# When the third chunk's down groups are woven into quarters 8 to 10: eight weight loads two units later, in both layers

## The chip, the cores and the metric

The kernel runs on one core of a Trainium2 chip. Five engines work from instruction queues of their own: TensorE (PE; its weight loads are shown as PEld), VectorE (DVE), ScalarE (ACT), GpSimd (POOL) and SyncE (SP, which here only issues DMAs). The metric is the time of one launch in microseconds (us) on the device.

## The reference

Two layers over a sequence of 256 tokens and 2048 channels, in float32. Layer 0 mixes tokens by causal pooling, layer 1 by dilated causal attention; each is followed by a layer norm, a gated feed-forward network with a causal convolution of width 3, and another layer norm. The change touches the feed-forward part of both layers and, a little, the attention's mask.

```
def conv_ffn(h, w_up, conv_w, conv_b, w_down):
    u = h @ w_up
    up = jnp.pad(u, ((0, 0), (CONV_WIDTH - 1, 0), (0, 0)))
    c = conv_b + up[:, 0:S] * conv_w[0]
    for j in range(1, CONV_WIDTH):
        c = c + up[:, j:j + S] * conv_w[j]
    gate, val = jnp.split(c, 2, axis=-1)
    return (jax.nn.silu(gate) * val) @ w_down
```

The inner width is 5504 columns. The attention has three branches, of window and dilation (128, 1), (512, 4) and (2048, 16); a mask says which of a query's keys each branch reads.

## The kernel before

**Numbers.** Every float32 weight is taken apart into a high part (wh, an ACT copy with rounding) and a low part (wl, a DVE subtraction), and so are the activations. A product is then the sum of three products of parts. This is called a split here, and each load of weights (raw, 1 MB from HBM) needs one: `do_split`, lines 82 and 83.

**Units.** The program is a list of units, each one load of weights with its matmuls. `run_units` walks the list: for unit i it issues the load of unit i+5 on SP (there are 3 buffers for raw weights, so a load waits until DVE has finished with an older one), emits the splits up to unit i+3 on ACT and DVE (4 buffers), then the unit's matmuls, then whatever earlier units left for "n units later" (`later`), then what follows the end of a group (`post`). Each engine works its queue in that order, so a DVE instruction that waits holds every later one on DVE.

**Up units.** The inner width is cut into quarters of 512 columns, 0 to 10; quarter 10 has 384. A quarter's gates are a group of four up units (`up`, over four blocks of 512 input rows), and its values another four. PE multiplies with lines 165 and 166. At a group's end DVE and ACT take the sums out of PSUM (`evac`, lines 578 and 579), ACT and DVE work the convolution's taps (lines 587, 592 and 593), and after the values DVE multiplies with the gates (line 684), splits the product (gq, lines 286 and 290) and makes sums of its blocks (`left_sums`, lines 646 to 660).

**Down units.** The down projection runs in four chunks of quarters: 0 to 2, 3 to 5, 6 and 7, and 8 to 10. For a chunk there are four down groups, one for each 512 output columns. Where the quarter has block sums (in chunk three both 6 and 7 have), one load serves a Strassen-like product of seven block products instead of eight. Such a load makes a pair of units "a" and "b", here called one K unit: PE works 42 matmuls with lines 227 to 229, and `split_sums` needs lines 103 to 109 for the first half and 96 and 97 for the second. At the end of a down group `early_post` and `tm_post` take its sums out of PSUM (lines 825 to 858), and POOL adds three pieces to the stream HT in SBUF by accumulating DMAs (line 271). In layer 0 a DVE transpose of HT follows three units after a down group of the third chunk (`to_features`, line 811), and then 16 small DMAs on SP.

**Weaving.** `weave` puts the K units of a down group between the up units of a group. In the third chunk a down group has two K units (quarters 6 and 7), and they follow the second and the fourth up unit. The four down groups go with the values of 8, the gates and values of 9, and the gates of 10. The product of quarter 9 is held back until the last K unit is done (`free[9]`), since its buffers belong to quarters 6 and 7. In layer 1 the last chunk needs the block sums of quarter 9 as well, at once with its second unit.

**The mask.** In the attention stage `masks(i)` makes block i of two small tables, 128 by 128 each, with one POOL iota and ten DVE instructions, 7, 8 and 9 units after the stage's start. Blocks 0 and 2 are the same.

Of the kernel before, what the change touches and what calls it, by code (L numbers as in the profile page):

```python
# [32 lines left out]
def trunk(ctx: ExitStack, tc: tile.TileContext, x, pool_w_in, pool_w_grp, pool_scale, pool_w_out,  # L33
# [3 lines left out]
    V, A, PE = nc.vector, nc.scalar, nc.tensor  # L37
# [14 lines left out]
    units = []  # L52
# [243 lines left out]
    H, XC, XP, ST = {}, {}, {}, {}  # L296
# [251 lines left out]
    def ffn(lay):  # L548
# [153 lines left out]
        def up(q):  # L702
            nb = min(4, NF - 4 * q)
            x0 = q == 0
            mode = "x" if x0 else "ab"
            mark = len(units)
            group(w_up, rows4, 512 * q, nb * P, psrcs if x0 else xsrcs, gate_post(q, nb, mode),
                  mode=mode)
            group(w_up, rows4, FF + 512 * q, nb * P, xsrcs, val_post(q, nb, "ab"))
            us = units[mark:]  # L710
            del units[mark:]
            return us[:4], us[4:]

        def weave(us, ks):
            items = []
            for k in ks:
                if len(k) > 3 and k[3] == "b":
                    items[-1].append(k)
                else:
                    items.append([k])  # L720
            ends = []
            for i, u in enumerate(us):
                units.append(u)
                j = i - 1 if len(items) > 2 else (i - 1) // 2 if i % 2 else -1
                if j >= 0:
                    units.extend(items[j])
                    ends.append(len(units) - 1)
            return ends

        def down(n, last):  # L730
# [16 lines left out]
        for n in (0, 1):  # L747
            d = down(n, False)
            q = chunks[n + 1][0]
            ends = [weave(us, ks) for us, ks in zip(up(q) + up(q + 1), d)]  # L750
# [3 lines left out]
                for us in up(q + 2):  # L754
                    units.extend(us)
        d = down(2, False)
        gates8, vals8 = up(8)
        units.extend(gates8)
        gates10, vals10 = up(10)
        for us, ks in zip((vals8,) + up(9) + (gates10,), d):  # L760
            free[9] = weave(us, ks)[-1]
        units.extend(vals10)
        mark = len(units)
        if lay == 0:
            rows = [(512 * q, min(512, FF - 512 * q)) for q in (8, 9, 10)]
# [76 lines left out]
    def tm_post(lay, n, c):  # L842
# [92 lines left out]
        return post  # L935

    ffn(0)
    marks.append(len(units))

# [215 lines left out]
    with tc.tile_pool(name="attn", bufs=1) as ap:  # L1155
        pools["attn"] = ap
        for nm in ("cnt", "negm"):
            ST[nm] = ap.tile([P, 3, P], F32, name=nm)

        def masks(i):  # L1160
            two = ap.tile([P, 2, P], F32, name="dist", tag="t1", bufs=2)
            dist, fm = two[:, 0], two[:, 1]
            nc.gpsimd.iota(dist, pattern=[[-1, P]], base=P * (i == 1), channel_multiplier=1,
                           allow_small_or_imprecise_dtypes=True)
            itwo = ap.tile([P, 2, P], I32, name="idist", tag="t1", bufs=2)
            idist, im = itwo[:, 0], itwo[:, 1]
            cn = ST["cnt"][:, i, :]
            V.tensor_copy(idist, dist)
            V.tensor_scalar(cn, dist, float(P), None, op0=OP.is_le)
            for dil in (4, 16):  # L1170
                V.tensor_scalar(im, idist, dil - 1, None, op0=OP.bitwise_and)
                V.tensor_copy(fm, im)
                V.scalar_tensor_tensor(cn, fm, 0.0, cn, op0=OP.is_equal, op1=OP.add)
            V.scalar_tensor_tensor(cn, dist, 0.0, cn, op0=OP.is_ge, op1=OP.mult)
            V.tensor_scalar(ST["negm"][:, i, :], cn, 0.0, NEG, op0=OP.is_equal, op1=OP.mult)

        for i in range(3):
            later(7 + i, lambda i=i: masks(i))
        run_units(marks[2])
    with tc.tile_pool(name="ffn1", bufs=4) as fp:  # L1180
# [31 lines left out]
```

## Time and profile before

| | |
|---|---|
| median of three runs | 2059.56 us (2056.8 to 2061.82) |
| the profiled execution | 2057.01 us |
| its span, first to last instruction | 2055.2 us |
| PE busy | 2027.2 us |
| DVE busy | 1687.6 us |
| ACT busy | 1257.2 us |
| mean granted clock of PE | 0.998 |
| layer 0, quarters 8 to 10 | 698.9 to 877 us of the span |
| layer 1, quarters 8 to 10 | 1811 to 1983.5 us of the span |

The engines' lines give busy time over the whole span. A line of the waits says who waited, for whom, how long in total, how often, and the longest in us. A line of the timeline has start, length, engine, source line, operation and names (out<-in), and in brackets the idle time ahead of it and who ended it. A line of the window table has a stretch, its length, and for each engine its busy time and instructions; then the share of the clock that PE was granted, and the DMA's share and rate.

### The profile page before, as it was taken

The page shows a single profiled execution, that of the slowest core. Times are in us where ns is not written, and L with a number is a line of the kernel's source. Part 1 is how long each engine was busy: PE and PEld are TensorE (multiplying, and loading weights), DVE is VectorE, ACT ScalarE, POOL GpSimd, SP SyncE. Part 2 cuts the span into 40 slices and gives each one's busy share as a digit, 9 for nine tenths or more (in the row PEclk, how much of TensorE's full clock was granted, in tenths as well). Part 3 has the DMA queues.
Part 4 walks back from the last instruction along what each step waited for, and adds up shares of the span by engine and source line. Part 5 has one row for each costly group of instructions (what it writes and reads, how often), then busy time and mean ns, then how long its engine had stood idle before and what let it go on. Part 6 is the DMA issues. An engine that isn't in the chain of part 4 may idle for free. (4 is left out here: it accounts for less than half of the span.)

```text
span 2055.2 us, 31252 instructions
## 1 busy us (share of the span) xinstructions
PE 2027.2 (99%) x12532; PEld 1810.4 (88%) x12532; DVE 1687.6 (82%) x2020; ACT 1257.2 (61%) x1689; POOL 75.2 (4%) x112
## 2 busy tenths in 40 slices
PE   9999999999999999999999999999999999999998
PEld 8999988899899988889888888998899888988987
DVE  6768877898889899889856667787889888988989
ACT  6445687666766675657444444477666677657663
POOL 2000000000000100100000000000001000000100
PEclk9999999999999999999999999999999999999999
DMA  8655567556666647775566555557666756656665
GB/s 272 211 186 191 172 200 212 193 191 221 195 195 211 207 167 197 220 231 172 167 217 191 176 176 166 183 185 226 184 197 191 228 185 196 206 193 199 196 211 184
DMA packets 278305, 405.92 MB, mean 198 GB/s; under 512 B 80414, under 2 KB 95668, under 8 KB 277904
## 3 DMA queue, kind: packets, MB, share of 16 engines
q1 hardware_dynamic: 266144, 389.72, 57.5%
q0 software_dynamic: 11584, 13.55, 4.4%
q8 instruction: 98, 1.61, 0.3%
q10 hardware_dynamic: 432, 0.66, 0.1%
q14 instruction: 47, 0.39, 0.1%
HBM read 380.01 MB, written 2.10 MB: 186 GB/s over the span
## 5 line engine op out<-in xcount | busy, mean ns | idle before, releaser
L165 PE MATMUL acc<-xc,wh 128*128 128x512 f32 x3264 | 1155.8, 396 | 2.2 <-DVE o L1061 1.2
L166 PE MATMUL acc<-xc,wl 128*128 128x256 f32 x3264 | 918.9, 282 | 12.1 <-DVE wl L83 12.1
L83 DVE TENSOR_TENSOR wl<-raw,wh 128x2048 fp32r<-128x2048 f32 (+2 forms) x318 | 687.6, 2168 | 259.5 <-ACT wh L82 257.4
L165 PEld LDWEIGHTS acc<-xc,wh 128*128 128x128 f32 x3264 | 617.4, 189 | 146.1 <-DVE o L1061 1.9
L82 ACT CAST wh<-raw 128x2048 fp32r<-128x2048 f32 (+2 forms) x318 | 573.0, 1809 | 195.0 <-PE acc L165 110.0
L166 PEld LDWEIGHTS acc<-xc,wl 128*128 128x128 f32 x3264 | 616.9, 189 | 16.3 <-DVE wl L83 15.8
L96 ACT CAST wh<-raw 128x1024 fp32r<-128x1024 f32 x116 | 121.7, 1053 | 153.8 <-DVE raw L107 133.5
L97 DVE TENSOR_TENSOR wl<-raw,wh 128x1024 fp32r<-128x1024 f32 x116 | 138.9, 1222 | 1.1 <-ACT wh L96 1.1
L103 ACT CAST wh<-raw 128x1024 fp32r<-128x1024 f32 x116 | 90.6, 830 | 41.7 <-DMA raw<-in_ffn_w_down_dram 27.3
L106 DVE TENSOR_TENSOR wl<-raw,wh 128x1024 fp32r<-128x1024 f32 x116 | 105.6, 952 | 3.0 <-ACT wh L103 2.6
L578 ACT COPY ut<-acc 128x256 f32<-128x256 f32 x164 | 52.9, 372 | 80.2 <-DVE u L579 60.2
L587 ACT ACTIVATE c<-u,cv 128x256 f32<-128x256 f32 x172 | 89.5, 594 | 19.1 <-DVE f L650 9.0
L227 PE MATMUL t<-wh,g 128*128 128x256 f32 x344 | 96.8, 282 | 0.0
L228 PE MATMUL t<-wl,g 128*128 128x256 f32 x344 | 96.7, 281 | 0.0
L229 PE MATMUL t<-wh,g 128*128 128x256 f32 x344 | 96.3, 280 | 0.0
L228 PE MATMUL s<-wl,xs 128*128 128x256 f32 x308 | 86.2, 280 | 2.2 <-DVE wl L97 2.2
L229 PE MATMUL s<-wh,xs 128*128 128x256 f32 x308 | 85.9, 279 | 0.0
L227 PE MATMUL s<-wh,xs 128*128 128x256 f32 x308 | 85.8, 279 | 0.0
L271 POOL DMA_DIRECT2D ht<-w x24 | 20.3, 847 | 1756.9 <-ACT wh L103 950.4
L592 ACT ACTIVATE a<-u,cv 128x256 f32<-128x256 f32 x172 | 73.5, 500 | 15.9 <-DVE g L660 6.5
L592 ACT ACTIVATE u<-u,cv 128x256 f32<-128x256 f32 x172 | 73.5, 499 | 0.0
L109 DVE TENSOR_TENSOR raw<-raw 128x1024 f32<-128x1024 f32 x58 | 71.1, 1225 | 2.0
(276 smaller groups left out, 3432.9 us busy)
## 6 DMA issues: line engine op xcount, KB each, us to landing
raw<-in_ffn_w_up_dram SPq DMA_DIRECT2D x160, 1024.0 KB, 4.9
raw<-in_ffn_w_down_dram SPq DMA_DIRECT2D x80, 1024.0 KB, 5.2
raw<-in_pool_w_out_dram SPq DMA_DIRECT2D x16, 1024.0 KB, 5.0
raw<-in_shared_w_k_dram SPq DMA_DIRECT2D x16, 1024.0 KB, 5.0
raw<-in_attn_w_q_dram SPq DMA_DIRECT2D x16, 1024.0 KB, 5.4
raw<-in_shared_w_v_dram SPq DMA_DIRECT2D x16, 1024.0 KB, 5.4
raw<-in_attn_w_o_dram SPq DMA_DIRECT2D x16, 1024.0 KB, 5.0
raw<-in_pool_w_in_dram SPq DMA_DIRECT2D x12, 1024.0 KB, 5.9
```

Source lines behind the costliest of these rows:

```text
L82: A.copy(wh[i][:, s], r[:, s])
L83: V.tensor_tensor(wl[i][:, s], r[:, s], wh[i][:, s].bitcast(F32), OP.subtract)
L96: A.copy(h[:, :, n], r[:, :, n])
L97: V.tensor_tensor(l[:, :, n], r[:, :, n], h[:, :, n].bitcast(F32), OP.subtract)
L103: A.copy(h[:, k, n], r[:, k, n])
L106: V.tensor_tensor(l[:, k, n], r[:, k, n], h[:, k, n].bitcast(F32), OP.subtract)
L165: PE.matmul(ps[m], h[:, k, c], q[:, k, :, :T], start=st, stop=False)
L166: PE.matmul(ps[m][:, :T], l[:, k, c], q[:, k, 0, :T], start=False, stop=sp and not shifted)
L227: PE.matmul(to, xh, h[:, k, n], start=opens and kk == 0, stop=False)
L228: PE.matmul(to, xh, l[:, k, n], start=False, stop=False)
L229: PE.matmul(to, xl, h[:, k, n], start=False, stop=ends and kk == 1)
L592: A.activation(to[:, m, :], u[:, m, i:i + T], AF.Copy, scale=cv[:, i, j:j + 1])
```

## The change

The weave of a down group of two K units now puts them ahead of the first and of the third up unit instead of behind the second and the fourth. Quarter 8's gates and values run without any K unit, and the four down groups go with the gates and values of 9 and of 10. The chunks of three items (chunks one and two) keep their order. In the attention stage the third mask block is no longer computed, but copied from the first by two ACT copies.

```diff
+            def put(item):
+                units.extend(item)
+                ends.append(len(units) - 1)
+
             for i, u in enumerate(us):
+                if len(items) == 2 and i % 2 == 0:
+                    put(items[i // 2])
                 units.append(u)
-                j = i - 1 if len(items) > 2 else (i - 1) // 2 if i % 2 else -1
-                if j >= 0:
-                    units.extend(items[j])
-                    ends.append(len(units) - 1)
+                if len(items) > 2 and i > 0:
+                    put(items[i - 1])
             return ends
...
         d = down(2, False)
-        gates8, vals8 = up(8)
-        units.extend(gates8)
-        gates10, vals10 = up(10)
-        for us, ks in zip((vals8,) + up(9) + (gates10,), d):
+        for us in up(8):
+            units.extend(us)
+        for us, ks in zip(up(9) + up(10), d):
             free[9] = weave(us, ks)[-1]
-        units.extend(vals10)
...
+            if i == 0:
+                for nm in ("cnt", "negm"):
+                    A.copy(ST[nm][:, 2, :], ST[nm][:, 0, :])
+
-        for i in range(3):
+        for i in range(2):
             later(7 + i, lambda i=i: masks(i))
```

On SP, where quarter 8 of layer 0 begins to be loaded, the loads stood so before (raw is the buffer of one unit's weights, w_up an up unit, w_down a K unit):

```order
L72 DMA raw_6849<-in_ffn_w_up_dram 128x4x512
L72 DMA raw_6907<-in_ffn_w_up_dram 128x4x512
L72 DMA raw_6961<-in_ffn_w_down_dram 128x4x512
L72 DMA raw_7051<-in_ffn_w_up_dram 128x4x512
L72 DMA raw_7114<-in_ffn_w_up_dram 128x4x512
L72 DMA raw_7163<-in_ffn_w_down_dram 128x4x512
```

and stand so now, from the same load on:

```order
L72 DMA raw_6849<-in_ffn_w_up_dram 128x4x512
L72 DMA raw_6907<-in_ffn_w_up_dram 128x4x512
L72 DMA raw_6961<-in_ffn_w_up_dram 128x4x512
L72 DMA raw_7005<-in_ffn_w_up_dram 128x4x512
L72 DMA raw_7053<-in_ffn_w_down_dram 128x4x512
L72 DMA raw_7156<-in_ffn_w_up_dram 128x4x512
L72 DMA raw_7205<-in_ffn_w_up_dram 128x4x512
L72 DMA raw_7250<-in_ffn_w_down_dram 128x4x512
```

The first K unit's load stands two loads of w_up later; from there on one K load follows every two up loads, as before.

On DVE, around the K unit in the middle of quarter 10's gates in layer 0, this stood before (wl is a low part of weights, c a convolution's sum, w and u the down group's pieces on their way to ht):

```order
L109 TENSOR_TENSOR raw_7994<-raw_7994 128x4x256
L593 TENSOR_TENSOR c<-c,a 128x1024
L826 TENSOR_TENSOR w<-w,s_7885 128x256
L827 TENSOR_TENSOR u_8120<-w,s_7886 128x256
L831 TENSOR_TENSOR w<-w,s_7886 128x256
L832 TENSOR_TENSOR u_8124<-u_8120,s_7886 128x256
L853 TENSOR_TENSOR ht<-ht,t_7883 128x512
L858 TENSOR_TENSOR ht<-ht,t_7884 128x256
L97 TENSOR_TENSOR wl_8135<-raw_7994,wh_8134 128x4x256 x2
L593 TENSOR_TENSOR c<-c,u 128x1024
L684 TENSOR_TENSOR c<-c 128x1024
L83 TENSOR_TENSOR wl_8176<-raw_8078,wh_8175 128x1536
```

and this stands there now, with the transpose that comes ahead of the K unit:

```order
L814 STREAM_TRANSPOSE hb<-ht 128x2x4x128
L104 TENSOR_TENSOR raw_7917<-raw_7917 128x2x256
L106 TENSOR_TENSOR wl_8005<-raw_7917,wh_8004 128x4x256
L106 TENSOR_TENSOR wl_8005<-raw_7917,wh_8004 128x2x256
L107 TENSOR_TENSOR raw_7917<-raw_7917 128x2x256
L109 TENSOR_TENSOR raw_7917<-raw_7917 128x4x256
L593 TENSOR_TENSOR c<-c,a 128x1024
L97 TENSOR_TENSOR wl_8053<-raw_7917,wh_8052 128x4x256 x2
L593 TENSOR_TENSOR c<-c,u 128x1024
L684 TENSOR_TENSOR c<-c 128x1024
L83 TENSOR_TENSOR wl_8099<-raw_8002,wh_8098 128x1536
```

The six instructions that take a down group out of PSUM (lines 826 to 858) are gone from between the two halves of this K unit's split; the transpose (line 811, in the new file 814) stood behind the next up splits and now stands ahead of the first half. Those six instructions now stand in the K unit between the gates of 10 and its neighbours, on DVE ahead of its second half:

```order
L109 TENSOR_TENSOR raw_7763<-raw_7763 128x4x256
L829 TENSOR_TENSOR w<-w,s_7634 128x256
L830 TENSOR_TENSOR u_7865<-w,s_7635 128x256
L834 TENSOR_TENSOR w<-w,s_7635 128x256
L835 TENSOR_TENSOR u_7869<-u_7865,s_7635 128x256
L856 TENSOR_TENSOR ht<-ht,t_7632 128x512
L861 TENSOR_TENSOR ht<-ht,t_7633 128x256
L97 TENSOR_TENSOR wl_7880<-raw_7763,wh_7879 128x4x256 x2
L83 TENSOR_TENSOR wl_7920<-raw_7829,wh_7919 128x1536
```

The instructions are the same, their numbers of lines in the new file are higher by three.

## The prediction

> **What bounds the kernel now.** I read the page's first part, then PE's waits in the two stretches that the change re-orders, then the clock there, and last the order of time on DVE where PE waits.
>
> ```profile
> span 2055.2 us, 31252 instructions
> PE 2027.2 (99%) x12532; PEld 1810.4 (88%) x12532; DVE 1687.6 (82%) x2020; ACT 1257.2 (61%) x1689; POOL 75.2 (4%) x112
> ```
>
> PE works 2027.2 of 2055.2 us. The change keeps every matmul, so all it can move is in the 28 us of idle time and in slow matmuls. The next two fences are PE's waits from the first up unit of quarter 8 on, in layer 0 (698.86 to 877 us) and in layer 1 (1811 to 1984 us); columns are us in total, times, longest.
>
> ```profile
> PE acc L166 <- DVE wl L83: 5.1, 3, 2.0
> PE s L228 <- DVE wl L97: 2.0, 3, 1.6
> PE s L227 <- DVE u L579: 1.6, 1, 1.6
> PE acc L165 <- ACT wh L82: 0.5, 1, 0.5
> ```
> ```profile
> PE acc L166 <- DVE wl L83: 5.3, 4, 1.8
> PE s L227 <- DVE u L579: 1.5, 1, 1.5
> PE acc L165 <- ACT wh L82: 0.5, 1, 0.5
> PE s L228 <- DVE wl L97: 0.2, 1, 0.2
> ```
>
> That is 9.2 and 7.5 us: more than half of PE's idle time lies in these two stretches, nearly all of it behind DVE's splits of weights (wl). Two stretches of half clock come on top (window table: stretch, length, busy PE, PEld, DVE, ACT, POOL, granted clock, DMA):
>
> ```profile
> 743.60:747.00 3.40, 3.40 (x13) 2.92 (x12) 3.40 (x3) 3.24 (x7) 0.00 (x0) 0.50 0.87 307
> 846.00:849.40 3.40, 3.40 (x13) 2.82 (x12) 2.75 (x4) 1.57 (x2) 0.00 (x0) 0.50 0.83 249
> 1854.90:1858.30 3.40, 3.40 (x20) 3.00 (x21) 3.40 (x3) 3.40 (x7) 0.00 (x0) 1.00 0.70 235
> ```
>
> Each costs half of its 3.4 us and counts as busy: 3.4 us together, in layer 0 alone; the third row, behind layer 1's longest wait, keeps the full clock. Just ahead of the second one PE does this:
>
> ```profile
> 845.30 0.39 PE L166 MATMUL acc<-xc,wl 128*128 128x256 f32 x1 [1.98 <-DVE wl L83]
> 845.53 0.40 PE L165 MATMUL acc<-xc,wh 128*128 128x512 f32 x1
> ```
>
> The first matmul lasts 0.39 us but the next starts 0.23 after it; matmuls overlap by 0.16 us, and each wait loses that beside its idle time. With 8 waits in layer 0 the pool is 9.2 + 3.4 + 8 x 0.16 = 13.9 us, with 7 in layer 1 it is 7.5 + 1.1 = 8.6 us; 22.5 us in all.
>
> **Why PE waits there.** DVE in layer 0 around the K unit that now follows the second up unit of quarter 10's gates:
>
> ```profile
> 830.31 0.69 DVE L104 TENSOR_TENSOR raw<-raw 128x512 f32<-128x512 f32 x1 [2.06 <-DMA raw<-in_ffn_w_down_dram]
> ...
> 835.12 1.22 DVE L593 TENSOR_TENSOR c<-c,a 128x1024 f32<-128x1024 f32 x1
> 836.25 0.41 DVE L826 TENSOR_TENSOR w<-w,s 128x256 f32<-128x256 f32 x1
> ...
> 838.83 2.35 DVE L97 TENSOR_TENSOR wl<-raw,wh 128x1024 fp32r<-128x1024 f32 x2
> 841.10 1.22 DVE L593 TENSOR_TENSOR c<-c,u 128x1024 f32<-128x1024 f32 x1
> 842.35 1.23 DVE L684 TENSOR_TENSOR c<-c 128x1024 f32<-128x1024 f32 x1
> 843.50 3.42 DVE L83 TENSOR_TENSOR wl<-raw,wh 128x1536 fp32r<-128x1536 f32 x2
> ```
>
> The weights land at 830.3 after DVE sat idle for 2.06 us; from there DVE runs without a pause: first half's split (to 835.1), a tap, the evacuation of the down group that ended one K unit earlier (836.25 to 838.83, 2.58 us), the second half's split, tap, product, and the split for the next up unit, ready only at 845.2, which is where PE stood. So the K unit in mid-group carries two chains at once; the one between groups carries no evacuation. Unit lengths on PE (two up units, two small ones of quarter 10, one K unit):
>
> ```profile
> 760.37:771.61 11.24, 11.24 (x67) 9.81 (x66) 11.03 (x15) 9.85 (x17) 1.56 (x3) 1.00 0.36 122
> 827.54:835.96 8.42, 8.42 (x51) 7.35 (x49) 5.92 (x7) 6.12 (x11) 0.00 (x0) 1.00 0.77 238
> 771.61:776.55 4.94, 4.94 (x45) 4.94 (x43) 4.91 (x4) 2.00 (x2) 1.03 (x2) 1.00 1.03 223
> ```
>
> So 5.62, 4.21 and 4.94 us. Two more of DVE's prices, quarter 10's up split and the transpose, grouped by form from 760 to 860 us (busy us, mean ns | idle before):
>
> ```profile
> L83 DVE TENSOR_TENSOR wl<-raw,wh 128x1536 fp32r<-128x1536 f32 x6 | 10.5, 1756 | 2.6 <-ACT wh L82 2.5
> L811 DVE STREAM_TRANSPOSE hb<-ht 128x1024 f32<-128x1024 f32 x3 | 3.7, 1242 | 0.7 <-issue 0.7
> ```
>
> **The change, part by part.** The up units keep their order (quarters 8, 9, 10, gates then values). Each of the eight K units of the third chunk moves two up units later, in both layers. Nothing is added or removed on PE. On SP each K unit's load of 1 MB moves behind two loads of w_up, in layer 0 the 16 copies that follow each transpose move too, and on POOL the three accumulates of each down group; their number stays. Two effects follow: the first K unit meets quarter 8 after eight plain up units, and a down group now ends in mid-group, so that its evacuation stands ahead of the K unit between groups and no longer ahead of the one in mid-group.
>
> *The first K unit.* In layer 0 it costs the 1.6 us wait on u L579 (the evacuation of quarter 8's gates), 0.5 on ACT, 0.2 on L97 and the 1.8 on L83, 4.1 us of idle, 0.6 for four waits, and a half-clock stretch of 1.7: 6.4. In layer 1 the same four rows without the clock: 4.6. There DVE has the left sums of quarters 6 and 7, the evacuation and this K unit's split in one queue:
>
> ```profile
> 728.23 0.68 DVE L104 TENSOR_TENSOR raw<-raw 128x512 f32<-128x512 f32 x1
> ...
> 734.17 1.07 DVE L579 TENSOR_TENSOR u<-acc,ut 128x256 f32<-128x256 f32 x3
> ...
> 740.41 2.29 DVE L83 TENSOR_TENSOR wl<-raw,wh 128x2048 fp32r<-128x2048 f32 x1 [2.36 <-ACT wh L82]
> ```
>
> The split moves 11.2 us of PE time later, behind up units that need 2.29 us of DVE each in 5.62. I take all 11.0 us as gone; at worst 2 us of it stays, as ACT's share.
>
> *K units in mid-group.* The evacuation leaves the front: L97 would start 2.58 us earlier, at 836.25, and its first half be ready at 837.4, when PE asks for it about 2.1 us into a K unit that began at 835.96: that wait goes. The next split would be ready at 842.6, and PE asks at 835.96 + 4.94 = 840.9: 1.7 us stay. In layer 0 a transpose (1.24 us) moves ahead of this first half's split; the 2.06 us of idle time can hide it, or not: 1.7 to 2.9, taken 2.3, where the 1.6 and 2.0 us in the rows stood (3.9 with the overlaps). A K load that lands late, as the 2.06 us at 830.3 shows, can come back; it is the upper end of this bound. The half clock here followed 1.6 and 2.0 us within 6 us; with one wait left I count its 1.7 as gone, and the other bound is that it stays. What is left of the rows, 0.2 and 1.3 us in layer 0 (the K unit in quarter 9's values) and 2.1 in layer 1 (5.3 less the 1.8 and 1.4 at the two ends of the stretch), are waits in mid-group too and fall to nothing by the same 2.58. Quarter 10's values get such a K unit for the first time: behind it stand short chains only, no product (1.23) and smaller taps, so 842.6 becomes about 840.9: 0 to 1.2, taken 0.3.
>
> *K units between groups.* PE's rows hold no wait at these, so they had room, whose size no row gives, and now carry the 2.58. Three of the four are affected (the first follows no down group). Below nothing this can't go, since no wait is there to take away; above, all 2.58 could show: 0 to 2.6 each, nearer to 0 since DVE also has less to do in mid-group, just ahead. I take 0.3 each in full groups and up to 1.0 ahead of quarter 10's values: 1.2 in layer 0, where a transpose leaves that stretch, and 1.6 in layer 1.
>
> *The end of layer 1.* The K units now end two small units (8.4 us) ahead of the last chunk instead of four (16.8). Before, on DVE and then on PE (the last chunk's first matmul, and the third of quarter 10's first product):
>
> ```profile
> 1959.36 2.41 DVE L97 TENSOR_TENSOR wl<-raw,wh 128x1024 fp32r<-128x1024 f32 x2
> ...
> 1968.33 1.76 DVE L83 TENSOR_TENSOR wl<-raw,wh 128x1536 fp32r<-128x1536 f32 x1 [1.98 <-ACT wh L82]
> ...
> 1974.13 0.96 DVE L593 TENSOR_TENSOR c<-c,a 128x768 f32<-128x768 f32 x1 [1.44 <-ACT a L592]
> ...
> 1990.59 0.75 DVE L579 TENSOR_TENSOR u<-acc,ut 128x256 f32<-128x256 f32 x2
> ...
> 1999.12 0.95 DVE L286 TENSOR_TENSOR g<-c,g 128x768 fp32r<-128x768 f32 x1
> ```
> ```profile
> 1983.46 0.39 PE L238 MATMUL t<-wh,g 128*128 128x512 f32 x1
> ...
> 2000.16 0.47 PE L240 MATMUL t<-wh,g 128*128 128x512 f32 x1
> ```
>
> The low part of quarter 10's product is ready at 2000.07 and PE uses it at 2000.16: no room. From the end of the last K split (1961.8) to the end of the evacuation of quarter 10's values (1991.3) are 29.5 us; less the idle 1.98 and 1.44, two small splits (3.5) and one evacuation (1.1) that now come ahead, 21.5 us of DVE work are left. At 841.2 less 2.58 a mid-group K split would end 2.6 us into its K unit; with the shorter chains here I estimate 0 to 2. From the unit's start PE needs 4.94 + 8.42 = 13.4 us to the last chunk. So the evacuation ends 8.1 to 10.1 us (21.5 + 0 to 2 - 13.4) into that chunk where it was 7.9 (1991.3 less 1983.5): 0.2 to 2.2 us of new wait, taken 1.2. In exchange the wait in quarter 10's values, one of the four in the 5.3 us, is counted as gone: DVE's tail there now falls into the last chunk. Layer 0's last chunk has no left sums and asks for quarter 10 three full units after its values: nothing.
>
> *The mask.* One of three blocks of ten small DVE instructions and an iota goes, two ACT copies come. PE waits for nothing there:
>
> ```profile
> ACT qt L975 <- DVE dist L1172: 6.5, 1, 6.5
> ```
>
> ACT stands idle for 6.5 us right there, so the copies' wait for DVE queues nothing that PE needs. That wait spans two blocks, so one block is worth 3.2 us of DVE at most, and as much could be lost if the copies held ACT's next cast. I take 0, since no row has PE waiting there.
>
> **Sum.** Layer 0: 13.9 less 2.3 + 0.3 + 1.2 = 10.1 gained. Layer 1: 8.6 less 0.3 + 1.6 + 1.2 = 5.5 gained. Together 15.6 us. The profiled execution took 2057.0 us, which is 2.6 under the median of the runs, 2059.6. So 2041.4 for it, and 2044 for the median.
>
> The Trainium skill, TensorE: Matmul & The Clock Gate, HAM oscillation, says that only idle gaps over about 3.4 us drop the clock. Here it dropped after waits of 1.8 and 2.0 us and held after one of 1.8 us in layer 1, so the rows decide. By the page the 2.3 us that I leave at quarter 10 could cost no clock, which is what I counted; by the rows it may cost 1.7 more.
>
> **The rivals.** (1) DVE stays the bound and the waits re-form. Quarter 10's two groups now both carry K units, with 4 x 4.21 + 2 x 4.94 = 26.7 us of PE; DVE needs for the first four splits of 1.76, two K splits of 6.8 (4.4 and 2.4 at 830 to 841), evacuation 2.6, transpose 1.2, two taps and a product of 1.2: 28 us; a wait of 2 us or more at either brings half clock back. For it: the 1.98 us wait above. Against: after eight plain up units DVE can have this chunk's first K split and an up split done, 9 us ahead. Then 4 to 10 us are gained: about 2052. (2) All DVE slack is enough: all waits go, 22 us, 2037. (3) The tail and the crossings between groups eat it: same within 0.2% (4 us, about what the runs can tell), 2060. (4) Slower: the transposes of layer 0 now stand right ahead of a K unit's split, and they wait for POOL's accumulates:
>
> ```profile
> 869.73 0.84 POOL L271 DMA_DIRECT2D ht<-w  x1 [28.03 <-issue]
> 878.04 1.25 DVE L811 STREAM_TRANSPOSE hb<-ht 128x1024 f32<-128x1024 f32 x1 [0.96 <-DMA ht<-u]
> ```
>
> They land 8.3 us after POOL's first issue. In the new order DVE has 7 to 8 us of work up to there (a second-half split, two up splits, an evacuation), so 0 to 1 us each. Were they to land 15 us after, each of the four would hold DVE 6.7 us more: 27 lost against 15.6 gained, 2071; it decides from about 12 us on. The Trainium skill, SBUF — State Buffer, SBUF: two separate sides, speaks for it: DVE instructions with two SBUF inputs shut out a GpSimd that reads SBUF, and DVE runs such splits back to back here. But POOL's first issue takes 0.84 us with DVE busy.
>
> **How the numbers follow.** My forecast, 10 to 22 us gained: 0.60. Rival 1: 0.15. Rival 2: 0.04. Rival 3: 0.07. Rival 4: 0.14. Faster by over 0.2%: 0.60 + 0.15 + 0.04 = 0.79; same 0.07; slower 0.14. The range from 2035 to 2056 holds the forecast, rival 1 and part of rival 2, 0.78; the forecast's own is 2038 to 2050.
>
> **What would show it.** Right: in the stretches of quarters 8 to 10 PE's waits fall from 9.2 and 7.5 us to 3 to 5 each, no wait on u L579, no half clock; the largest wait of layer 0 lies in quarter 10's gates, and one near 1 us at quarter 10's first product in layer 1's last chunk. Wrong: waits over 2 us between groups, a transpose waiting several us for ht, or a half clock in either stretch.

## The result, and the profile after

The changed kernel takes 2048.88 us (median of five runs, 2047.83 to 2051.56) against 2059.56 for the kernel before (five runs beside it, 2056.8 to 2061.82): 10.7 us less. The ratio is 0.9952, with a 95% interval of 0.9938 to 0.9967; taken by the ratio the gain is 9.9 us (6.8 to 12.8). The forecast was 15.6. So it is faster, by about two thirds of what the sum gave.

The profiled execution after took 2051.56 us, the slowest of its five, and the one before was 2.6 us under its median. Their spans differ by only 5.4 us. Of this, layer 0 gained 4.6 us (PE's matmuls between 707 and 896 us of the span before, 188.7 us, take 184.1 after) and layer 1 gained 2.4 us (the matmuls between 1838 and 2005 us, 167.2 us, take 164.8). Against that, the first thousand matmuls, which the change does not touch, took 1.2 us more (154.7 and 155.9 us; between 154.6 and 157.9 in the traces of all the kernels here), and the rest of the kernel 0.4 us more. The runs decide on the size, and the traces say where it comes from.

The engines' lines of the page after:

```profile
span 2049.8 us, 31251 instructions
PE 2025.5 (99%) x12532; PEld 1809.4 (88%) x12532; DVE 1684.2 (82%) x2010; ACT 1259.6 (61%) x1691; POOL 74.9 (4%) x111
```

PE's waits after, in layer 0 from 700 to 877 us of the span and in layer 1 from 1808 to 1990 (us in total, times, longest):

```profile
PE acc L166 <- DVE wl L83: 2.8, 3, 2.0
PE s L228 <- DVE wl L97: 2.6, 2, 1.5
PE acc L165 <- DVE w L829: 1.1, 1, 1.1
PE acc L165 <- DVE u L835: 0.7, 1, 0.7
```
```profile
PE t L229 <- DVE xs3Q L660: 1.9, 1, 1.9
PE s L228 <- DVE wl L97: 1.2, 2, 0.9
PE acc L166 <- DVE wl L83: 0.5, 1, 0.5
```

That is 7.2 and 3.6 us where 9.2 and 7.5 stood. The row on u L579, the evacuation ahead of the first K unit, is gone in both layers, and wl L83 has lost 2.3 us in layer 0 and 4.8 in layer 1. Three rows are new: PE waits for the evacuation of a down group (w L829, u L835) at layer 0's last chunk, and for quarter 9's block sums (xs3Q L660) at layer 1's.

Where the long waits lie on PE, in layer 0 and then in layer 1 (the idle time is in brackets):

```profile
827.70 0.39 PE L228 MATMUL s<-wl,xs 128*128 128x256 f32 x1 [1.11 <-DVE wl L97]
832.90 0.38 PE L166 MATMUL acc<-xc,wl 128*128 128x256 f32 x1 [1.99 <-DVE wl L83]
...
858.79 0.39 PE L228 MATMUL s<-wl,xs 128*128 128x256 f32 x1 [1.52 <-DVE wl L97]
862.47 0.39 PE L166 MATMUL acc<-xc,wl 128*128 128x256 f32 x1 [0.45 <-DVE wl L83]
...
872.53 0.50 PE L165 MATMUL acc<-g,wh 128*128 128x512 f32 x1 [1.08 <-DVE w L829]
873.84 0.50 PE L165 MATMUL acc<-g,wh 128*128 128x512 f32 x1 [0.69 <-DVE u L835]
```
```profile
1983.44 0.38 PE L229 MATMUL t<-wh,xs3Q 128*128 128x256 f32 x1 [1.93 <-DVE xs3Q L660]
```

The first pair is the K unit in the middle of quarter 10's gates with the up unit behind it, the second pair the same in quarter 10's values, the third is the last chunk. No wait lies at a K unit between two groups, in either layer.

Two stretches of the window table (length, busy PE, PEld, DVE, ACT, POOL, granted clock, DMA), one just behind the wait of 1.99 us in layer 0 and one behind that of 1.93 us in layer 1:

```profile
833.00:836.40 3.40, 3.40 (x20) 2.99 (x21) 2.65 (x3) 1.52 (x3) 0.00 (x0) 1.00 1.08 305
...
1984.90:1988.30 3.40, 3.40 (x18) 3.40 (x17) 3.40 (x6) 3.18 (x6) 0.00 (x0) 0.50 0.37 100
```

The clock held after the first and halved after the second, which costs half of the 3.4 us, 1.7 us, as the prediction counts it. With 0.16 us for each wait, layer 0 is left with 7.2 + 7 x 0.16 = 8.3 us, layer 1 with 3.6 + 4 x 0.16 + 1.7 = 5.9. The forecast left 3.8 and 3.1 us.

### The profile page after: what moved, and what is told of

The parts are those of the page before. It is cut to its first block, busy times and chain, and to the rows that moved or that the text cites. A ratio compares the mean times of both kernels' runs of the same rounds, so it can differ in the third digit from the quotient of the medians.

```text
span 2049.8 us, 31251 instructions
## 1 busy us (share of the span) xinstructions
PE 2025.5 (99%) x12532; PEld 1809.4 (88%) x12532; DVE 1684.2 (82%) x2010; ACT 1259.6 (61%) x1691; POOL 74.9 (4%) x111
## 3 DMA queue, kind: packets, MB, share of 16 engines
q8 instruction: 98, 1.61, 0.3%
## 5 line engine op out<-in xcount | busy, mean ns | idle before, releaser
L83 DVE TENSOR_TENSOR wl<-raw,wh 128x2048 fp32r<-128x2048 f32 (+2 forms) x318 | 687.5, 2168 | 259.1 <-ACT wh L82 258.7
L97 DVE TENSOR_TENSOR wl<-raw,wh 128x1024 fp32r<-128x1024 f32 x116 | 138.4, 1221 | 0.0
```

The lines of the kernel that those rows point to most:

```text
L83: V.tensor_tensor(wl[i][:, s], r[:, s], wh[i][:, s].bitcast(F32), OP.subtract)
L97: V.tensor_tensor(l[:, :, n], r[:, :, n], h[:, :, n].bitcast(F32), OP.subtract)
```

## The experiments

All were timed over several rounds against the kernel before on the same chip. "Under before" is worked out from the ratio: (1 - ratio) x 2059.6 us, by which the changed kernel is 9.9 us under. The intervals reach 1.8 to 3 us to either side, so two kernels within some 4 us of each other are not told apart.

| kernel | median, us | ratio to before (95%) | under before, us |
|---|---|---|---|
| changed kernel | 2048.88 | 0.9952 (0.9938 to 0.9967) | 9.9 |
| e_lay0, layer 0 alone | 2052.55 | 0.9966 (0.9953 to 0.9978) | 7.0 |
| e_lay1, layer 1 alone | 2057.68 | 0.9982 (0.9973 to 0.9990) | 3.7 |
| e_mask, third block computed | 2050.46 | 0.9956 (0.9942 to 0.9970) | 9.1 |
| e_late, K units two later | 2062.51 | 1.0011 (1.0002 to 1.0020) | -2.3 |
| e_hold, last chunk's split later | 2048.04 | 0.9944 (0.9931 to 0.9958) | 11.5 |
| e_free, quarter 9's product earlier | 2052.29 | 0.9962 (0.9949 to 0.9974) | 7.8 |
| e_both, hold and free | 2052.47 | 0.9966 (0.9952 to 0.9979) | 7.0 |
| e_turn, transposes behind the K unit | 2051.34 | 0.9965 (0.9951 to 0.9978) | 7.2 |
| e_sums, block sums a group later | 2052.68 | 0.9967 (0.9955 to 0.9978) | 6.8 |
| e_all, hold, turn and sums | 2054.26 | 0.9972 (0.9964 to 0.9981) | 5.8 |
| e_half, K loads of half the size | 2050.96 | 0.9961 (0.9947 to 0.9974) | 8.0 |
| e_notr, no transposes in layer 0 | 2047.62 | 0.9941 (0.9929 to 0.9954) | 12.2 |

### Each layer alone: e_lay0 and e_lay1

The new order in one layer, the old weave in the other; with False as its third argument `weave` puts the K units behind the second and fourth up unit (for e_lay1 the test is `lay == 1`):

```diff
-        for us in up(8):
-            units.extend(us)
-        for us, ks in zip(up(9) + up(10), d):
-            free[9] = weave(us, ks)[-1]
+        gates8, vals8 = up(8)
+        units.extend(gates8)
+        if lay == 0:
+            units.extend(vals8)
+            for us, ks in zip(up(9) + up(10), d):
+                free[9] = weave(us, ks)[-1]
+        else:
+            gates10, vals10 = up(10)
+            for us, ks in zip((vals8,) + up(9) + (gates10,), d):
+                free[9] = weave(us, ks, False)[-1]
+            units.extend(vals10)
```

> The changed order of quarters 8 to 10 in layer 0 alone; layer 1 is woven as before; the mask block is copied. The changed kernel's median is 10.7 us under the one before. By the wait rows of its profile layer 0 gave 3 to 4 us there, and 1.7 to 3.4 more by the two half-clock stretches of before, layer 1 the rest. If the gains of the layers are independent, as I think: 5 to 7 us under before, with no wait of PE behind the third-chunk evacuation of quarter 8 in layer 0 and the old waits in layer 1. If the gain were a matter of the clock alone (layer 0 only has such stretches in the profile of before): 10 us, and nothing left for layer 1.

> The changed order in layer 1 alone. If the layers add up: 4 to 5 us under before, and together with the run of layer 0 alone within 2 us of 10.7. If the tail of layer 1 eats what its middle gains (the profile after shows 2.2 us of idle time and half a clock stretch there): 0 to 2 us under before.

Layer 0 alone is worth 7.0 us and layer 1 alone 3.7. Their sum of 10.7 agrees with the 9.9 of the whole change within the intervals: the layers add up, and each gives about two thirds of its forecast (10.1 and 5.5). So no single place swallowed the rest; something is left over in both.

### The mask: e_mask

```diff
-            if i == 0:
-                for nm in ("cnt", "negm"):
-                    A.copy(ST[nm][:, 2, :], ST[nm][:, 0, :])
-
-        for i in range(2):
+        for i in range(3):
             later(7 + i, lambda i=i: masks(i))
```

> The changed kernel with the third mask block computed again instead of copied. My theory: the mask is worth nothing, since PE waits for nothing near it, so 10 to 11 us under before, as the changed kernel. Rival: the 2 us of DVE time that it frees ahead of the first scores counts, then 8 to 9 us under before.

With the third block computed again the ratio is 0.9956 against 0.9952: no difference that these runs can tell. The gain is that of the order.

### How early must the K units stand: e_late

Quarter 8 goes alone as in the change, but the K units stand behind the second and fourth up unit, two up units later. Quarter 9's product is released by the last group's first K unit, and its own block sums have a buffer of their own, since without that the buffers run out:

```diff
             for i, u in enumerate(us):
-                if len(items) == 2 and i % 2 == 0:
-                    put(items[i // 2])
                 units.append(u)
+                if len(items) == 2 and i % 2 == 1:
+                    put(items[i // 2])
...
-            free[9] = weave(us, ks)[-1]
+            free[9] = weave(us, ks)[0]
...
-                own = apart()
+                o9 = fp.tile([P, 2, 2, P], F32R, name="xs3", tag="xsd", bufs=1)
+                own = [o9[:, 0], o9[:, 1]]
```

> Quarter 8 goes alone, but the down units keep their old place behind the second and fourth up unit of the gates and values of 9 and 10: every one is two up units later than in the changed kernel, and the evacuation of a down group is again ahead of the one in mid-group. Quarter 9's product is released one K unit earlier than in the changed kernel and its own block sums have a buffer of their own, since there are not enough buffers otherwise. My theory is that the first K unit's relief and the place of the evacuation each bring a part. Then the waits in mid-group are back (2 to 4 us in each layer) and the tail is worse, since the last K unit ends just ahead of the last chunk: 2 to 6 us under before. Rival: only the relief of quarter 8 counts, and this is as fast as the changed kernel, 10 to 11 us under before.

This is 2.3 us slower than before: against my theory, and against the rival as well. PE's waits in e_late, in layer 0 (700 to 877 us) and in layer 1 (1808 to 2003 us):

```profile
PE s L228 <- DVE wl L97: 3.7, 3, 1.6
PE acc L166 <- DVE wl L83: 2.4, 2, 2.0
PE t L227 <- DVE w L830: 1.6, 1, 1.6
```
```profile
PE s L228 <- DVE wl L97: 3.7, 3, 1.5
PE t L239 <- DVE wl L83: 3.5, 1, 3.5
PE acc L166 <- DVE wl L83: 2.0, 1, 2.0
PE t L239 <- DVE u L563: 1.4, 1, 1.4
```

The row on u L579 is gone here too, so eight up units ahead of the first K unit are enough for that wait. What the place within the group does shows in the middle of quarter 10's gates in layer 1: the evacuation (L830 to L862) stands again ahead of the K unit's second half, and PE waits 0.59 + 1.99 us where the changed kernel does not wait. But e_late differs from the changed kernel in a second thing: its last K unit ends right ahead of the last chunk. PE waits 1.4 + 1.5 + 3.5 us in layer 1's last chunk (1.5 of it in the row on wl L97) and, past the end of the first window, 0.25 + 1.88 us in layer 0's. So the room that quarter 8 gives is not enough by itself; how much of the loss is the place and how much the later end was not measured apart. e_free, below, has the early release of the product alone; it is 2.1 us behind the changed kernel by the ratios, e_late 12.2.

### The last chunk: e_hold, e_free, e_both

DVE at the start of layer 0's last chunk in the changed kernel:

```profile
868.72 2.29 DVE L83 TENSOR_TENSOR wl<-raw,wh 128x2048 fp32r<-128x2048 f32 x1 [3.87 <-ACT wh L82]
870.93 1.22 DVE L286 TENSOR_TENSOR g<-c,g 128x1024 fp32r<-128x1024 f32 x1
872.07 0.41 DVE L829 TENSOR_TENSOR w<-w,s 128x256 f32<-128x256 f32 x1
```

DVE stands idle for 3.87 us for the last chunk's first load (issued on SP at 860.31, it landed at 866.70, and ACT's cast, which DVE waits for, began at 866.78), and the split of quarter 9's product (L286) and the last evacuation (L829), for which PE waits, are queued behind it. e_hold emits that split one unit later, so that it comes behind both:

```diff
+    held = set()
...
-        while state["split"] < min(len(units), i + n + 1):
+        while state["split"] < min(len(units), i + n + 1) and not (state["split"] in held and i < state["split"] - 2):
...
         mark = len(units)
+        held.add(mark)
```

> The changed kernel with one difference: the split of the last chunk's first unit is emitted two units ahead of its matmuls and not three, so that it stands on DVE and ACT behind the release of quarter 9's product, its block sums and the last down group's evacuation, and no longer ahead of them. My theory: the waits at the start of the last chunk (in the profile after, PE stops 2.9 us in layer 0 for the last evacuation, start to start, and 2.5 us and half a clock stretch in layer 1 for quarter 9's block sums) come from this split, which waits for its load (DVE idle 3.9 and 2.2 us) with that work queued behind it. Then both go or nearly so: 3 to 6 us faster than the changed kernel, 14 to 17 us under before. Rival: DVE has too much work there whatever its order; then 0 to 1 us faster than the changed kernel, the waits move to the split of the first or second unit of the last chunk.

e_free releases quarter 9's product earlier, at the last group's first K unit (the second and third piece of e_late's diff, in the changed kernel's order). e_both has these two pieces and e_hold's edit.

> The changed kernel with quarter 9's product released behind the second to last K unit and not behind the last one (its block sums get a buffer of their own for that), so that 4.4 us of DVE work in layer 1, 1.2 in layer 0, moves from the tail ahead of the K unit in the middle of quarter 10's values, where DVE sat idle for 2.2 us waiting for a load. My theory: layer 1's wait for the block sums goes with its half clock, 3 to 4 us; layer 0's wait for the evacuation shrinks by about 1 us; the K unit in quarter 10's values gets up to 1.5 us worse in layer 1. Net 2 to 4 us faster than the changed kernel, 13 to 15 us under before. Rival (too much DVE work whatever its order): the wait at that K unit grows by as much as the tail loses, 0 to 1 us.

> Both at once. By my theory they aim at the same tail, so the sum is less than the parts: 4 to 6 us faster than the changed kernel, 14 to 17 us under before. By the rival (too much DVE work whatever its order) no better than 1 us under the changed kernel.

PE's waits in the same two stretches, of e_hold (its lines are one higher):

```profile
PE acc L167 <- DVE wl L84: 3.0, 3, 2.0
PE s L229 <- DVE wl L98: 2.2, 2, 1.2
```
```profile
PE t L240 <- DVE wl L84: 1.2, 2, 1.0
PE s L229 <- DVE wl L98: 1.0, 2, 0.7
PE acc L167 <- DVE wl L84: 0.5, 1, 0.5
```

The waits for the evacuation and the block sums are gone in both layers. So the reading of the queue is right: these waits came from the split that stood ahead. But some of that time is now a wait for the split itself: the two rows on wl L84 are 3.0 us in layer 0 (2.8 before the edit) and 1.2 us new in layer 1. The stretches lose 5.2 and 2.7 us instead of 7.2 and 3.6. The time, 11.5 us under before, is not told apart from the changed kernel's 9.9, and 3 to 6 us more had been expected.

In e_free the price appears at the K unit in the middle of quarter 10's values. PE in layer 1, and DVE ahead of it:

```profile
1963.30 0.38 PE L227 MATMUL s<-wh,xs 128*128 128x256 f32 x1 [3.76 <-ACT wh L96]
1964.56 0.58 PE L228 MATMUL s<-wl,xs 128*128 128x256 f32 x1 [0.88 <-DVE wl L97]
```
```profile
1953.40 0.69 DVE L104 TENSOR_TENSOR raw<-raw 128x512 f32<-128x512 f32 x1 [2.06 <-DMA raw<-in_ffn_w_down_dram]
...
1957.09 1.23 DVE L109 TENSOR_TENSOR raw<-raw 128x1024 f32<-128x1024 f32 x1
1958.23 1.22 DVE L286 TENSOR_TENSOR g<-c,g 128x1024 fp32r<-128x1024 f32 x1
```

The product and its sums now stand between the halves of a K unit whose load came late anyway, and PE waits 3.76 and 0.88 us there where it waited 0.92. In layer 0, at the same K unit, it waits 2.56 us where it waited 1.52. Both e_free and e_both fell short of what was expected: work taken from the end of the stretch is missed in its middle.

### The two largest waits left: e_turn, e_sums, e_all

e_turn moves layer 0's transposes behind the K unit in mid-group; e_sums asks for quarter 9's block sums in the last chunk's second down group in place of its first (the expectation's parenthesis names quarter 10's values groups by mistake; the groups are the last chunk's down groups); e_all has both and e_hold's edit.

```diff
-                later(3, lambda: to_features(c))
+                later(5, lambda: to_features(c))
```
```diff
-            sevens[9] = (0, 2)
+            sevens[9] = (1, 2)
```

> The changed kernel, with layer 0's transposes of the fourth feature block moved behind both halves of the K unit that stands in the middle of quarter 10's gates. My theory: layer 0 waits there (1.27 us at the K unit and 2.15 us at the next up unit in the profile of after, and the clock halves there in some executions) because the transposes stand ahead of the K unit's split and wait for GpSimd's load (0.7 and 2.2 us); layer 1 has no transposes there and no wait. Then both waits go, but for about 0.5 us, and the time is 3 to 5 us under that of the changed kernel, so 13 to 16 us under the kernel before. The rival: VectorE has more work there than the stretch of two groups holds, whatever its order; then the waits only move behind the transposes, to the split of the next up unit, and the time is within 1 us of the changed kernel, 10 to 11.5 us under before.

> The changed kernel, with quarter 9's block sums in layer 1 asked for one group later (in quarter 10's second values group and not in its first). My theory: the wait of 2.08 and 0.44 us that the last groups of layer 1 make for the block sums, with the half clock of 3.4 us behind it (1.7 us lost), is there because TensorE reaches their transposes before VectorE has got to them, while VectorE is late by the 2.2 us that it waited for the last chunk's first load. Then this wait goes and the time is 2 to 4 us under that of the changed kernel, 12.5 to 15 us under before. The rival: VectorE is as late for whatever stands next, and the wait goes to the split of the last chunk's next unit; then the time is within 1 us of the changed kernel.

> Three edits to the changed kernel at once: the transposes behind the K unit in layer 0, the block sums a group later in layer 1, and the split of the last chunk's first unit behind quarter 9's product instead of ahead of it. If each takes away a wait of its own, 5 to 8 us come off the changed kernel, 15.5 to 19 us under before. If VectorE's total work between the loads is what is late, the waits move on from place to place and the sum is that of the best single edit, 0 to 2 us under the changed kernel.

None is shown to be faster than the changed kernel. By the ratios e_all is 4.1 us slower than it, just past what the runs can tell; e_turn and e_sums, 2.7 and 3.1 us behind, are not told apart from it. PE's largest wait at or behind an edited place, in e_turn in quarter 10's gates, in e_sums in layer 1's last chunk and in e_all in layer 0's last chunk:

```profile
831.72 0.38 PE L166 MATMUL acc<-xc,wl 128*128 128x256 f32 x1 [2.66 <-DVE wl L83]
```
```profile
1994.12 0.79 PE L240 MATMUL t<-wh,g 128*128 128x512 f32 x1 [3.36 <-DVE g L286]
```
```profile
891.52 0.50 PE L166 MATMUL acc<-g,wh 128*128 128x512 f32 x1 [2.69 <-DVE g L287]
```

In e_turn the K unit in the gates waits no longer (1.11 before the edit), and PE waits 2.66 us for the split behind it instead of 1.99. In quarter 10's values, whose transpose moved as well, 1.52 + 0.45 us became 0.20 + 1.72 + 1.58. In e_sums the wait for the sums is gone, and quarter 10's product, which had no row of its own, is late by 3.36. In e_all PE still waits 2.48 us for the split in quarter 10's gates, and a new wait stands in layer 0's last chunk. In all three the work moved on DVE's queue, and the wait moved to what now stands last, as the rivals said; e_all did worse than its rival, which had 0 to 2 us under the changed kernel.

### Less work or a smaller load: e_notr and e_half

e_notr leaves layer 0's transposes to features out (the copies behind them read HT as it stands, so layer 1's input is in a wrong order):

```diff
-        hb = hp.tile([P, 4, T], F32, name="hb", tag="h")
-        hf = hb.rearrange("p m t -> p (m t)")
-        V.transpose(hf.rearrange("p (m t c) -> p t m c", m=4, t=2), HT[c].rearrange("p t (m c) -> p t m c", m=4))
+        hf = HT[c].rearrange("p t c -> p (t c)")
```

e_half loads two of the four row blocks of each K unit in the third chunk, and the splits read these twice; the core of it:

```diff
-        ks = pieces(i, nk)
+        ks = [slice(0, 2)] if units[i][4:] else pieces(i, nk)
...
+        parts = [(as_four(h[:, :, N1]), as_four(l[:, :, N1]), four(r11) if half else as_four(r[:, :, N1])),
+                 (h[:, B2, N2], l[:, B2, N2], r12 if half else r22)]
...
-        d = down(2, False)
+        d = [[k + (1,) if len(k) > 3 else k for k in g] for g in down(2, False)]
```

> The changed kernel without layer 0's four transposes to features (the copies behind them read HT as it stands, so layer 1 gets its input in a wrong order): DVE has 1.25 us less to do in each of four groups and doesn't wait there for GpSimd's pieces. Moving the transposes only moved the wait. My theory: DVE's work in quarter 10's gates is 1 to 2 us more than the stretch holds, and the transpose is that surplus; without it the waits of 1.27 and 2.15 us there fall to those of layer 1 (none), with the half clock that some executions have there: 3 to 5 us under the changed kernel, 13.5 to 16 us under before. The rival: the K unit's load is late by itself (it landed with DVE idle where the transposes had been moved away); then 0 to 1 us.

> The changed kernel, with the loads of the third chunk's eight K units in each layer cut to half (0.5 MB instead of 1 MB); the splits read the loaded half twice, so DVE and ACT work the same number of elements, and the down projection of quarters 6 and 7 is computed with wrong weights. What is taken away is about 2 us of each K unit's transfer. My theory: the waits that are left at the K units in the middle of quarter 10's groups (in the profile of after 1.27 and 2.15 us in layer 0's gates, 1.68 and 0.61 in its values, 1.07 and 0.61 in layer 1's values, 7.4 in all) come from K loads that land late, with DVE idle for 2.2 us ahead of the split. Then most of them go and the time is 4 to 7 us under that of the changed kernel, 15 to 18 us under before. The rival: DVE's work between those loads is what is late, and its idle time ahead of a split is only a piece that the queue had to spare; then the time is within 1.5 us of the changed kernel, 9 to 12 us under before.

e_notr is 12.2 us under before, not told apart from the changed kernel by the times. The traces differ where they should. PE's waits in e_notr in layer 0's stretch:

```profile
PE acc L166 <- DVE wl L83: 1.3, 2, 0.9
PE acc L165 <- DVE w L827: 1.1, 1, 1.1
PE s L228 <- DVE wl L97: 0.9, 1, 0.9
PE acc L165 <- DVE u L833: 0.7, 1, 0.7
```

The wait of 1.11 us at the K unit in quarter 10's gates is gone and that of 1.99 behind it is 0.88, though DVE still stood idle for 1.06 us there for the K unit's load. So DVE's work, with the transpose in it, is what is late in layer 0's gates: taking 1.25 us of it away shortened the two waits by 2.2, where moving it (e_turn) shortened them by 0.4. In quarter 10's values of layer 0 the waits without the transpose are 0.90 + 0.46 us, the same as the 0.92 + 0.45 that layer 1, which has none, shows in the changed kernel.

e_half was to tell how much a late load costs, and does not settle it. The K units' own loads, eight in layer 0 (727 to 846 us) and eight in layer 1 (1834 to 1950 us), first in the changed kernel and then in e_half (the last column is the median from issue to landing in us):

```profile
raw<-in_ffn_w_down_dram SPq DMA_DIRECT2D x8, 1024.0 KB, 6.1
raw<-in_ffn_w_down_dram SPq DMA_DIRECT2D x8, 1024.0 KB, 5.7
```
```profile
raw<-in_ffn_w_down_dram SPq DMA_DIRECT2D x8, 512.0 KB, 4.6
raw<-in_ffn_w_down_dram SPq DMA_DIRECT2D x8, 512.0 KB, 4.5
```

So 1.2 to 1.5 us was taken away, not 2; and since DVE overwrites what ACT still has to read twice, DVE's first step of each split (L112 there) now waited for ACT, 3.2 us over layer 0's stretch. The waits at the K units in the middle of quarter 10's groups were gone in this kernel, but that for the next split in the gates stayed at 1.7 us (1.99 in the changed kernel), new ones of about 1.3 us stood before splits in quarter 9, and the time, 8.0 us under before, is no better. Whether the late K loads in quarter 10's values cost PE time by themselves stays open. A fourth buffer for raw weights, so that these loads can be issued earlier, would test it directly; it was not tried.

## Why the prediction was right, and where its sum was off

The kernel is faster, inside the range, and by the mechanism named: the waits behind DVE's splits shrink because the first K unit now follows eight plain up units and a down group's evacuation no longer precedes the K unit in mid-group. The range, 2035 to 2056, held rival 1 (about 2052) as well, so the time alone does not choose between them; the traces and the experiments do. Of the 22.5 us in the two stretches the sum left 6.9. The rows of the profile after have 14.2 left, so 8.3 gone; PE's own progress through the two stretches gives 7.0 us, and the runs, which average over executions with and without half clock, 9.9 to 10.7. Step by step:

- **The first K unit** (all 11.0 us counted as gone): right. No row on u L579, and no wait at that K unit, in either layer.
- **K units in mid-group, quarter 10's gates** (2.3 us left in layer 0, nothing in layer 1): right in place, short in size: 1.11 + 1.99 and two overlaps of 0.16, 3.4 us; nothing in layer 1. The transpose that separates the layers was named, and e_notr confirms it. In quarter 9's gates, where the sum had left nothing, 0.37 us stayed in layer 0, behind the K unit in mid-group.
- **Quarter 10's values** (0.3 us left in each layer): mis-sized. It measured 1.52 + 0.45 + 0.32 = 2.3 us in layer 0, and 0.9 + 0.5 + 0.32 = 1.7 in layer 1. The step counted DVE's shorter chains and not DVE's idle time ahead of them; how much of the wait that idle time makes is not shown (e_half left it open). In layer 1 DVE had been through with its work and waited for the K unit's weights:

```profile
1951.14 1.75 DVE L83 TENSOR_TENSOR wl<-raw,wh 128x1536 fp32r<-128x1536 f32 x1
1955.15 0.69 DVE L104 TENSOR_TENSOR raw<-raw 128x512 f32<-128x512 f32 x1 [2.26 <-DMA raw<-in_ffn_w_down_dram]
```

  The prediction had said that such a load "can come back", but had put it into the bound of another term.
- **K units between groups** (1.2 and 1.6 us): too much. No wait there: these K units took on the 2.58 us of the evacuation without one. These 2.8 us hide part of what the other steps left out, which by the rows comes to 10 us.
- **Layer 0's last chunk** (nothing): wrong. Only quarter 10 was looked at. PE waited 1.08 + 0.69 us, with overlaps 2.1, for the last evacuation, queued behind a split for whose load DVE stood idle 3.87 us. e_hold took these waits away.
- **The end of layer 1** (1.2 us at quarter 10's first product): right chunk, wrong place, mis-sized: 1.93 + 0.28 us at quarter 9's block sums, 2.5 with overlaps, and 1.7 of half clock. e_hold's missing wait shows the same queue as the cause.
- **The clock** (no half clock left): wrong for layer 1 in this profile, and for layer 0 in others (below). A half clock in either stretch was one of the prediction's own signs of being wrong, and it came. The price of 1.7 us was a little high: 1.5 by the traces (below).
- **The mask** (0): nothing that the runs can tell.

The other signs came in part: layer 1's waits are within the 3 to 5 us that were named, layer 0's 7.2 are not; u L579 is gone and layer 0's largest wait lies in quarter 10's gates, but the wait in layer 1's last chunk is at the block sums and 1.93 us long.

Of the rivals the first, DVE staying the bound with waits that re-form, describes much of what is left: the gain lies at the border between its "4 to 10 us" and the forecast's 10 to 22. e_turn, e_sums and e_all showed it three times: the wait moves with the queue. The fourth rival, transposes that wait for POOL's pieces, was weak: two of the four waited, 0.70 us in quarter 10's gates and 2.23 us in its values:

```profile
819.83 1.25 DVE L814 STREAM_TRANSPOSE hb<-ht 128x1024 f32<-128x1024 f32 x1 [0.70 <-DMA ht<-u]
...
851.19 1.25 DVE L814 STREAM_TRANSPOSE hb<-ht 128x1024 f32<-128x1024 f32 x1 [2.23 <-issue]
```

With the transposes gone (e_notr) DVE stood idle at these two places all the same, for 1.06 and 2.23 us, for the K unit's load. No experiment gave a version shown to be faster than the changed kernel; e_hold may be, by 1.6 us at the ratio's face value.

## What to carry to other kernels

When a change shifts work on an in-order queue that is nearly full, count the queue's idle time for loads along with its work, and walk the queue to the very end of the stretch: what stands behind a late load there is late with it. Moving one item that PE waits for only names another item; taking work off the queue, or starting it earlier while there is still room, shortens the waits. Two such gains do not add up unless each has its own slack: here the two layers added up, and the three local edits at once lost time.

## What the runs showed of the hardware

The clock halved after waits far shorter than the half-clock stretch itself, and not every time. The wait for the split behind the K unit in quarter 10's gates of layer 0 is 1.98 or 1.99 us long in seven traces; the clock halved behind it in four of them (e_lay0, e_mask, e_sums, e_hold) and stayed full in three (the changed kernel, e_free, e_both). This is e_hold's:

```profile
832.13 0.58 PE L167 MATMUL acc<-xc,wl 128*128 128x256 f32 x1 [1.98 <-DVE wl L84]
```

The difference is where the wait falls. In all fourteen traces the granted clock changes only at steps of 3.41 us, which lie fixed within an execution: the two half-clock stretches of the profile before begin at 743.6 and 846.0 us, thirty steps apart. What decided, as far as these traces show, was how much of PE's idle time fell into one step. In the four traces it was 1.97 to 1.99 us, all or nearly all of the wait; in the other three the wait lay across two steps, with 1.71, 1.61 and 1.45 us in one of them. Here are the step with the wait and the step behind it, in the changed kernel and in e_hold (the busy time of PE is the second number, the clock the third from the end):

```profile
831.21:834.62 3.41, 1.72 (x10) 1.55 (x11) 3.31 (x2) 0.62 (x1) 0.00 (x0) 1.00 1.11 334
834.62:838.03 3.41, 3.41 (x21) 2.95 (x20) 2.73 (x4) 1.84 (x3) 0.00 (x0) 1.00 0.86 281
```
```profile
828.70:832.11 3.41, 1.45 (x12) 1.12 (x10) 3.38 (x4) 1.47 (x1) 0.00 (x0) 1.00 0.88 214
832.11:835.52 3.41, 3.39 (x11) 2.91 (x12) 2.21 (x2) 0.53 (x1) 0.00 (x0) 0.50 1.10 282
```

Over the fourteen traces, from 15 us on and up to PE's last matmul, every step at full clock with 1.83 us of idle time or more was followed by half clock (23 of 23), and none with 1.65 us or less; of the six between, two were.

The page TensorE: Matmul & The Clock Gate of the Trainium skill, in HAM oscillation, speaks of gaps over about 3.4 us; these rows do not agree, as the prediction had said of the profile before. The price shows in the same seven traces: the 60 matmuls behind that wait took 11.36 to 11.38 us with half clock and 9.84 or 9.85 without, so 1.5 us. The lesson for a sum: a wait near 2 us carries a chance of 1.5 us more, by where it falls, and two executions can differ by several such steps. Layer 0 is woven alike in the changed kernel, e_mask and e_sums, and their traces hold none, three and two steps of half clock there.

The other surprise was the load: with other loads on the way, 1 MB landed 5.7 to 6.1 us after its issue and 0.5 MB 4.5 to 4.6 us, so that half the size bought only about a quarter of the time.
